# Layer 0's value products: the first 512 tokens by single blocks, norm weights spread by TensorE, one product of column group 2 moved ahead of S1

## The chip, the cores and the metric

The kernel runs on one core of one Trainium2 chip. The metric is device time in microseconds (us) of one execution. The engines are TensorE (PE), VectorE (DVE), ScalarE (ACT), GpSimd (POOL) and SyncE (SP), which issues the DMA transfers in this kernel. Each engine works through its own list of instructions in turn; semaphores tie the lists together. "SBUF" is the on-chip working memory, "PSUM" the eight banks of 128 x 512 float32 that PE writes.

## The reference

Two decoder layers on 1024 tokens of width 1024, in float32. Layer 0 mixes tokens with dilated attention in three head groups, layer 1 with gated linear attention; each is followed by a squared-ReLU MLP. What this change touches is the very beginning: the first norm and the values of layer 0.

```python
def rmsnorm(x, w):
    xf = x.astype(jnp.float32)
    y = xf * lax.rsqrt(jnp.mean(xf * xf, axis=-1, keepdims=True) + NORM_EPS)
    return (y * w.astype(jnp.float32)).astype(x.dtype)

def dilated_attention(h, w_in, w_out):
    qkv = (h @ w_in).reshape(B, S, N_GROUPS, 3, ATTN_HEADS, HEAD_DIM)
    ...
    for g, (window, dil) in enumerate(DILATED_GROUPS):
        q = apply_rope(qkv[:, :, g, 0], cos, sin) * (HEAD_DIM ** -0.5)
        k = apply_rope(qkv[:, :, g, 1], cos, sin)
        v = qkv[:, :, g, 2].astype(jnp.float32)
...
def reference(x, ...):
    for i in range(DEPTH):
        h = rmsnorm(x, norm_mix_w[i])
        ...
```

## The kernel before

**Products.** Every float32 operand is cut into a rounded part (hi, `float32r`) and a remainder (lo). A product of two operands takes three matmuls (hi by hi, hi by lo, lo by hi). Large products are split into 2 x 2 blocks and done by a scheme with seven block products instead of eight, whose operands are sums and differences of blocks. For the values (class `Values`) A is the normalized x, transposed, in four blocks: `a11` and `a12` are the first 512 tokens with the first and second half of the 1024 features, and `a21`, `a22` (tiles `a` of half 1) the tokens from 512 on. S1 = A21 + A22, S2 = S1 - A11 and so on. B is one group's 1024 x 1024 of weights; there are three groups g. `Values` counts half products n: 14 for each group, q = (n mod 14) / 2 is the block product, m the half of the contraction. Product q uses the A operand `ORDER[q]` = a12, a11, s1, s2, s4, s3, a22, so that products 0 and 1 need a12, products 2 and 3 a11, products 4 and 5 S1, and products 14 and 15 again a12, with the weights of column group 2 (g = 1). One half product is 4 token blocks x 2 x 3 = 24 matmuls of 128x128 by 512 columns; `acc` holds its four PSUM banks, pB for q = 0, 2, 4, 6 and pA for the others. `product(n, blocks)` may do it for some of the token blocks.

**Weights.** `load(n)` issues a 512 KB transfer; `rounded(n)` makes the rounded part `dh` on ACT, `remain(n)` the remainder `dl` on DVE; `total(n)` first forms a difference on DVE where the scheme needs one. `copy` moves a PSUM bank to SBUF on ACT, `add` adds another bank to it on DVE and stores the result (`vscr`). `sums(n)` calls those that stand ahead of product n.

**x.** The 8 blocks of 128 tokens come in four pairs, tiles `x0`. `Halves.norm(p)` handles a pair: ACT squares each block with a sum (`junk`, L243); `rstd_of` works out the root for both at once, with Ln and Exp on ACT (L230, L231) and five small steps on DVE; then DVE scales with the norm weights into `xn` (L252). `turn(p)` transposes the pair on PE, four 128 x 128 blocks for one PSUM bank `pT` (L334), and ACT copies each bank to the tile `a` (L336). `cut(name, c)` then makes hi on ACT (L344) and lo on DVE (L346) from `a`, 256 tokens at a time. `sum1` forms S1 (L350). The norm weights come as one transfer that repeats the row on all 128 partitions (`load_norm_w`, L208), tile `wbc`.

**Order.** In this part of the program the order is written out by hand: the sequence of calls at the end of the excerpt below is the order in which each engine gets its instructions. It goes by pairs of blocks: pair 0 is normed, transposed and cut; products 0 to 2 run on blocks 0 and 1; pairs 1 and 2 are normed; pair 1 is transposed; product 3 runs on blocks 0 and 1; then products 0 to 3 on blocks 2 and 3, S1, and the rest, one whole half product after another. Tiles come from pools of fixed size with one tag each (`h8`, `k4`, `t2`, `sm`); a buffer is used again when its readers are done.

Of the kernel before, what the change touches and what calls it, by code (L numbers as in the profile page):

```python
# [9 lines left out]
F32 = mybir.dt.float32  # L10
F32R = mybir.dt.float32r
# [3 lines left out]
OP = mybir.AluOpType  # L15
# [26 lines left out]
def hybrid_trunk(ctx, tc, x, norm_mix, norm_mlp, norm_fin, a_in, a_out, g_in, g_up, g_b, g_nw,  # L42
# [702 lines left out]
    class Values:  # L745

        STEPS = 14 * NG
        small = False
        BLOCKS = ((1, 0), (0, 0), (0, 1), (1, 1), (1, 1), None, (1, 0))

        def __init__(self):
# [78 lines left out]
                                  stop=m == 1 and k == 1 and v == 2, skip_group_check=True)  # L830

        def copy(self, name, s, t, g):
            if name == "c22":
                if t % 2 == 0:
                    self.pair = k4([P, 2, 512], F32, "c22")
# [15 lines left out]
        def sums(self, n):  # L851
# [4 lines left out]
                    self.add("c21", "B", t, g - 1)  # L856
            for t in (2 * m, 2 * m + 1):
                if q == 1:
                    self.copy("c11", "B", t, g)
# [18 lines left out]
    class Mixed(Values):  # L878

        STEPS = 28  # L880
        small = True

        def __init__(self):
            super().__init__()
# [380 lines left out]
            at(t + 10, lambda half=half: join(half), 9)  # L1265


    x0 = []
    vals = Values()
    for p in range(NB // 2):  # L1270
        t = h8([P, 2, D], F32, "x0")
        for i in range(2):
            sp.dma_start(t[:, i, :], x[0, 256 * p + 128 * i:256 * p + 128 * i + 128, :])
        x0.append(t)
        if p == 0:
            wbc = load_norm_w(norm_mix[0])
            sp.dma_start(ident, ident_d)
            for n in range(4):
                vals.load(n)
    sp.dma_start(masks, msk)  # L1280
    hs = Halves(x0, wbc, vals, None)
    hs.norm(0, (512, 768, 0, 256), 256)
# [6 lines left out]
    hs.cut("a11", 0)  # L1289
    vals.prep(2)  # L1290
    vals.prep(3)
    hs.norm(1)
    for n in range(3):
        vals.product(n, [0, 1])
    hs.norm(2)
    hs.turn(1)
    vals.product(3, [0, 1])
    hs.cut("a12", 1)
    hs.cut("a11", 1)
    vals.load(4)  # L1300
    vals.load(5)
    hs.turn(2)
    hs.sum1(0)
    vals.total(4)
    hs.rstd(3)
    hs.norm(3)
    for n in range(2):
        vals.product(n, [2, 3])
    hs.cut("s1", 0)
    vals.rounded(4)  # L1310
    hs.turn(3)
    vals.remain(4)
    vals.product(2, [2, 3])
    vals.total(5)
    vals.sums(2)
    hs.sum1(1)
    hs.cut("s1", 1)
    vals.sums(3)
    vals.rounded(5)
    vals.product(3, [2, 3])  # L1320
    vals.remain(5)
    vals.load(6)
    vals.load(7)
    for c in range(2):
# [2 lines left out]
    hs.cut("s2", 0)  # L1327
    vals.rounded(6)
    hs.cut("s2", 1)
    vals.sums(4)  # L1330
    vals.sums(5)
    vals.remain(6)
    vals.load(8)
    vals.product(4)
# [16 lines left out]
            for c in range(2):  # L1351
                hs.cut("a22", c)
    vals.load(12)
    for n in range(8, vals.STEPS):
        if n == 12:
            ctab = h8([P, 2, S], F32, "tab")
            sp.dma_start(ctab[:, 0, :], tab[:, 0, :])
# [7 lines left out]
        if n == vals.STEPS - 1:  # L1365
            heads.stage(0, 2)
            heads.stage(0, 3)
        vals.sums(n)
        vals.prep(n + 2)
        vals.load(n + 5)  # L1370
        vals.product(n)
    for t in range(4):
        vals.add("c21", "B", t, NG - 1)
# [699 lines left out]
```

## Time and profile before

| | |
|---|---|
| time, median of 3 runs | 2618.7 us (2617.86 to 2620.56) |
| the profiled execution | 2618.82 us, span 2617.0 us |
| PE busy | 2590.2 us, 99% of the span |
| DVE, ACT busy | 1859.8 us (71%), 1277.1 us (49%) |
| first product of PE starts | 12.88 us after the span's start |

The profile comes from one execution. Times on its rows count from the span's start. A row of the timeline has the start, the duration, the engine, the line, the operation and the tiles (output, then inputs), and in brackets the idle time of the engine just before, with what ended it. A row of the groups has the busy time and the mean duration in ns after the bar, then idle time. A row of the windows has, for one stretch, the busy time of PE, of PE's weight loads, DVE, ACT and POOL with the number of instructions of each, then the granted share of PE's clock, the share of the DMA engines and GB/s. A row of the waits names who waited for whom: us in total, times, longest.

### The profile page before, as it was taken

The numbers are of one execution on the slowest core, as the hardware profiler recorded it, in microseconds if no ns is written. First come the engines' busy times: TensorE is split into PE (matmuls) and PEld (weight loads), VectorE is DVE, ScalarE is ACT, GpSimd is POOL, SyncE is SP. The second block draws the span as 40 slices with busy tenths as digits, with TensorE's granted clock in tenths as the row PEclk, the third lists the DMA queues.
The fourth block names the chain that finished last, engine by engine and source line by source line (L and its number), as shares of the span: only waits on it lengthen the run. The fifth ranks groups of instructions, "written<-read, shape, count | busy, mean of one in ns | idle before, by whom it ended". The sixth has DMA issues, their size and how long they took to land.

```text
span 2617.0 us, 33041 instructions
## 1 busy us (share of the span) xinstructions
PE 2590.2 (99%) x12144; PEld 2159.1 (83%) x12144; DVE 1859.8 (71%) x2986; ACT 1277.1 (49%) x2319; POOL 1.8 (0%) x7
## 2 busy tenths in 40 slices
PE   8999999999999999999999999999999999999998
PEld 6888888888888888888888888778888888888887
DVE  7645888888888768666657587877658866666566
ACT  6333455555555436555534345654326555553343
POOL 0000000000000000000000000000000000000000
PEclk9999999999999999999999999999999999999999
DMA  5534365655656733544775452462523544396543
GB/s 189 169 129 125 101 162 133 163 151 145 160 148 172 232 121 111 179 160 146 268 263 185 139 196 96 127 205 97 176 72 127 170 147 163 127 355 202 187 147 125
DMA packets 327010, 423.12 MB, mean 162 GB/s; under 512 B 19808, under 2 KB 192224, under 8 KB 326848
## 3 DMA queue, kind: packets, MB, share of 16 engines
q1 hardware_dynamic: 326848, 421.01, 51.0%
q8 instruction: 95, 1.56, 0.2%
q14 instruction: 67, 0.55, 0.1%
HBM read 279.71 MB, written 116.06 MB: 151 GB/s over the span
## 4 chain that ended last, share of the span: by engine, by line
PE 88%; DVE 7%; ACT 3%; issue 1%; DMA 1%; SPq 0%; ACTq 0%; DVEq 0%
PE pX L598 17%; PE pB L1578 13%; PE pV L598 11%; PE pA L1578 10%; PE pY L598 6%; PE pZ L598 6%; PE pB L829 5%; PE pd L215 3%; PE pd L214 3%; PE pd L213 3%; PE pA L829 3%; PE pS L976 2%; PE pO L1017 2%; DVE dl L814 1%; PE pP L1003 1%
## 5 line engine op out<-in xcount | busy, mean ns | idle before, releaser
L1578 PE MATMUL pB<-dh 128*128 128x512 f32 x512 | 199.4, 389 | 0.0
L1578 PE MATMUL pB<-dh,dl 128*128 128x512 f32 x512 | 199.2, 389 | 0.0
L1578 PE MATMUL pB<-dl,dh 128*128 128x512 f32 x512 | 199.2, 389 | 0.0
L222 DVE TENSOR_TENSOR dl<-sin,dh 128x1024 fp32r<-128x1024 f32 x112 | 136.5, 1219 | 45.9 <-ACT dh L219 45.3
L219 ACT ACTIVATE dh<-sin 128x1024 fp32r<-128x1024 f32 x112 | 117.9, 1052 | 91.0 <-PE pB L1578 32.2
L219 ACT ACTIVATE dh<-kept 128x1024 fp32r<-128x1024 f32 x64 | 67.9, 1061 | 182.5 <-DVE kept L1543 137.8
L598 PE MATMUL pV<-s4h,wd 128*128 128x512 f32 x448 | 150.8, 398 | 0.0
L1578 PE MATMUL pA<-dh,dl 128*128 128x512 f32 x384 | 149.4, 389 | 0.0
L1578 PE MATMUL pA<-dh 128*128 128x512 f32 x384 | 149.4, 389 | 0.0
L1578 PE MATMUL pA<-dl,dh 128*128 128x512 f32 x384 | 149.4, 389 | 0.0
L992 ACT ACTIVATE pt<-pt,orow 128x128 f32<-128x128 f32 (+1 forms) x192 | 84.8, 442 | 96.7 <-DVE orow L990 96.7
L1578 PEld LDWEIGHTS pB<-dl,dh 128*128 128x128 f32 x512 | 96.1, 188 | 20.0
L1578 PEld LDWEIGHTS pB<-dh,dl 128*128 128x128 f32 x512 | 96.1, 188 | 19.9
L1578 PEld LDWEIGHTS pB<-dh 128*128 128x128 f32 x512 | 96.1, 188 | 19.8
L536 DVE TENSOR_TENSOR wal<-raw,wah 128x512 fp32r<-128x512 f32 x112 | 76.2, 687 | 42.9 <-ACT wah L535 42.9
L607 ACT ACTIVATE c<-c 128x512 f32<-128x512 f32 x64 | 40.4, 632 | 122.7 <-DVE c L635 78.9
L598 PEld LDWEIGHTS pV<-s4h,wd 128*128 128x128 f32 x448 | 84.1, 188 | 17.8 <-DVE rb L623 0.3
L536 DVE TENSOR_TENSOR wbl<-t,wbh 128x1024 fp32r<-128x1024 f32 x56 | 68.6, 1225 | 38.4 <-ACT wbh L535 38.4
L222 DVE TENSOR_TENSOR dl<-kept,dh 128x1024 fp32r<-128x1024 f32 x64 | 78.3, 1224 | 24.5 <-ACT dh L219 18.6
L990 DVE CUSTOM_DVE_ANT_0 pt<-pS,masks 128x128 f32<-128x128 f32 (+1 forms) x192 | 58.2, 347 | 50.5 <-PE pS L976 50.5
L598 PE MATMUL pY<-a12h,wah 128*128 128x512 f32 x224 | 89.5, 400 | 0.0
L598 PE MATMUL pZ<-a22h,wgh 128*128 128x512 f32 x224 | 89.3, 399 | 0.0
(336 smaller groups left out, 7370.5 us busy)
## 6 DMA issues: line engine op xcount, KB each, us to landing
sin<-acts SPq DMA_DIRECT2D x112, 512.0 KB, 3.9
raw<-in_mlp_w_up_dram SPq DMA_DIRECT2D x64, 512.0 KB, 5.8
acts<-s SPq DMA_DIRECT2D x64, 512.0 KB, 3.4
raw<-in_mlp_w_down_dram SPq DMA_DIRECT2D x64, 512.0 KB, 4.7
raw<-in_attn_w_in_dram SPq DMA_DIRECT2D x96, 256.0 KB, 4.5
cw<-c SPq DMA_DIRECT2D x192, 128.0 KB, 2.3
acts<-c SPq DMA_DIRECT2D x64, 256.0 KB, 2.1
kept<-in_mlp_w_down_dram SPq DMA_DIRECT2D x32, 512.0 KB, 5.7
```

What stands on the lines that cost most here:

```text
L213: pe.matmul(ps, sh, mh, start=start, stop=False)
L214: pe.matmul(ps, sh, ml, start=False, stop=False)
L215: pe.matmul(ps, sl, mh, start=False, stop=stop)
L219: act.activation(hi, src, AF.Copy)
L222: dve.tensor_tensor(lo, src, hi.bitcast(F32), op=OP.subtract)
L536: self.remain(lambda: dve.tensor_tensor(lo, src, hi.bitcast(F32), op=OP.subtract))
L598: pe.matmul(st[b], u[:, k, :], v, start=first and k + n == 0, stop=k == 3 and n == 2, skip_group_check=True)
L829: pe.matmul(self.acc[s][t], a[:, c], b[:, k, :], start=fresh and m + k + v == 0, stop=m == 1 and k == 1 and v == 2, skip_group_check=True)
L976: pe.matmul(ps[:, i, :128 * n], self.qT[:, 128 * b:128 * b + 128], self.kT[:, k0:k0 + 128 * n], start=True, stop=True)
L990: dve.tensor_tensor_reduce(pt[:, i, :128 * n], ps[:, i, :128 * n], masks[:, m0:m0 + 128 * n], -scale, 1e38, op0=OP.add, op1=OP.min, accum_ ...
L992: act.activation(pt[:, i, :128 * n], pt[:, i, :128 * n], AF.Exp, scale=-1.0, bias=m, accum_out=self.row[:, r, HD:HD + 1])
L1578: pe.matmul(self.acc[s][t], a[:, k, c], b[:, k, :], start=fresh and m + k + v == 0, stop=m == 7 and k == 1 and v == 2, skip_group_check=True)
```

## The change

**Blocks.** The first 512 tokens are handled one block of 128 at a time. `root(b)` forms the reciprocal root of one block with two steps less on DVE; `normed(b, half)` scales one half of its features; `facing(b, half)` transposes this half, four 128 x 128 blocks into one bank, and ACT rounds hi straight from that bank. Its `rest()` makes lo on DVE from the bank as well, and then ACT copies the bank to `a`. Products 0 to 3 run block by block (`both`), and each block's c11 is copied and added at once.

**Norm weights.** The row of norm weights is loaded once, to one partition (`wrow`, 4 KB). PE spreads it over the partitions, two matmuls with a row of ones; DVE copies the two banks to `wbc`.

**Column group 2.** Products 14 and 15 (a12 by the weights of g = 1) run block by block after products 0 to 3, ahead of S1. Their results, c11 of g = 1, are copied at once to two pair tiles and kept until product 18. The list of the later steps (`plan`) leaves 14 and 15 out. Blocks 4 to 7 are transposed by `turn` as before, but their roots and scalings stand among these steps.

**Transfers.** Order before: blocks 0 and 1, the spread norm weights, ident, weights 0 to 3, the other blocks, masks. Now: block 0, the row of norm weights, ident, weights 0 to 2, block 1, weights 3, blocks 2 to 5, weights 14 and 15, blocks 6 and 7, masks. Weights 4 and 5 follow the stores of c11.

```diff
         def copy(self, name, s, t, g):
-            if name == "c22":
+            if name == "c22" or (name == "c11" and g == self.ahead):
...
+    def root(b):
+        r = root0[b] = sm([P, 5], "root")
+        ss, nv, t, y, z = (r[:, i:i + 1] for i in range(5))
+        junk = t2([P, D], BF16, "junk")
+        act.activation(junk, rows0(b), AF.Square, accum_out=ss)
+        dve.tensor_scalar(nv, ss, -0.5 / D, -0.5 * EPS, op0=OP.mult, op1=OP.add)
+        act.activation(t, ss, AF.Ln, scale=1.0 / D, bias=eps)
+        act.activation(y, t, AF.Exp, scale=-0.5)
+        dve.scalar_tensor_tensor(z, y, nv, y, op0=OP.mult, op1=OP.mult)
+        dve.scalar_tensor_tensor(z, z, 1.5, y, op0=OP.add, op1=OP.mult)
...
+    def facing(b, half):
+        ps = bank("pT").rearrange("p (k t) -> p k t", k=4)
+        for k in range(4):
+            c = 512 * half + 128 * k
+            pe.transpose(ps[:, k, :], xn0[b][:, c:c + 128], ident)
+        s, sl = vals.h[("a11", "a12")[half]], slice(128 * b, 128 * b + 128)
+        hi, lo = s.hi[0][:, :, sl], s.lo[0][:, :, sl]
+        act.activation(hi, ps, AF.Copy)
+
+        def rest():
+            dve.tensor_tensor(lo, ps, hi.bitcast(F32), op=OP.subtract)
+            act.activation(hs.a[0, half][0][:, :, sl], ps, AF.Copy)
+        return rest
...
+    for c in (512, 0):
+        ps = bank("pw")
+        pe.matmul(ps, ones[0:1, 0:P], wrow[0:1, c:c + 512], start=True, stop=True)
+        dve.tensor_copy(wbc[:, c:c + 512], ps)
+    root(0)
+    normed(0, 1)
     vals.rounded(0)
-    hs.turn(0, (2, 3))
+    rest = facing(0, 1)
     vals.remain(0)
-    hs.cut("a12", 0)
-    hs.turn(0, (0, 1))
-    vals.prep(1)
...
+    for b in range(1, 4):
+        rest = facing(b, 0)
+        both(0, b)
+        rest()
+        vals.add("c11", "A", b - 1, 0)
+        root(b + 1)
+        if b < 3:
+            normed(b + 1, 1)
+            rest = facing(b + 1, 1)
+            vals.copy("c11", "B", b, 0)
+            both(2, b)
+            rest()
+            normed(b + 1, 0)
+        else:
+            vals.rounded(14)
+            root(5)
+            normed(4, 1, 0)
+            vals.remain(14)
+            normed(5, 1, 0)
+            vals.copy("c11", "B", b, 0)
+            both(2, b)
+    hs.xn[2] = [xn0.pop(4), xn0.pop(5)]
+    hs.turn(2)
+    vals.prep(15)
+    root(6)
+    both(14, 0)
+    vals.add("c11", "A", 3, 0)
+    root(7)
+    normed(6, 1, 0)
+    hs.sum1(0)
+    normed(7, 1, 0)
+    hs.cut("s1", 0)
+    vals.copy("c11", "B", 0, 1)
+    both(14, 1)
...
-    for n in range(8, vals.STEPS):
+    plan = [*range(8, 14), *range(16, vals.STEPS), *range(vals.STEPS, vals.STEPS + 5)]
+    for i, n in enumerate(plan[:-5]):
```

The order of instructions at two places. On ACT, from the squares of one group of blocks to the copies after the next transposes, before (pT is a bank of transposes, junk the squares, t and y the root, a the transposed x; a bracket names the engines or transfers whose semaphores the row waits for):

```order
L243 ACTIVATE junk_258,ss_257<-x0_110 128x1024 [waits DMAHW2_49]
L243 ACTIVATE junk_260,ss_257<-x0_110 128x1024 [waits DMAHW3_49]
L230 ACTIVATE t_264<-v_262 128x2 [waits DVE_49]
L231 ACTIVATE y_263<-t_264 128x2 [waits Activation_49]
L336 ACTIVATE a_144<-pT_278 128x2x256 [waits PE_49]
L336 ACTIVATE a_145<-pT_284 128x2x256 [waits PE_49]
L336 ACTIVATE a_144<-pT_290 128x2x256 [waits PE_49]
L336 ACTIVATE a_145<-pT_296 128x2x256 [waits PE_49]
L344 ACTIVATE a12h_160<-a_145 128x4x256 [waits Activation_49]
L344 ACTIVATE a11h_180<-a_144 128x4x256
```

and now, one turn of the loop over blocks (b = 1):

```order
L1331 ACTIVATE a11h_128<-pT_234 128x4x128 [waits PE_49]
L1335 ACTIVATE a_130<-pT_234 128x4x128 [waits DVE_49]
L1310 ACTIVATE junk_257,root_256<-x0_94 128x1024 [waits DMAHW0_49]
L1312 ACTIVATE root_256<-root_256,eps_100 128x1 [waits Activation_49]
L1313 ACTIVATE root_256<-root_256 128x1 [waits Activation_49]
L1331 ACTIVATE a12h_126<-pT_266 128x4x128 [waits PE_49]
L840 ACTIVATE c11_272<-pB_164 128x512
L1335 ACTIVATE a_131<-pT_266 128x4x128 [waits DVE_49]
L1331 ACTIVATE a11h_128<-pT_289 128x4x128 [waits PE_49]
```

Before, the squares of pair 2 stand ahead of pair 1's transposes, and every copy of a bank waits for PE alone. Now the squares of block 2 stand behind the copy of block 1's bank, and that copy waits for DVE, whose remainder reads the same bank.

On DVE, the steps from the roots to the scaling of tokens from 512 on (v, t, y or root the reciprocal root, xn the scaled block, x0_110 and x0_95 the pair with blocks 4 and 5), before:

```order
L229 TENSOR_SCALAR v_262<-ss_257 128x2
L232 TENSOR_TENSOR t_264<-y_263 128x2
L233 TENSOR_TENSOR t_264<-t_264,v_262 128x2
L234 TENSOR_SCALAR t_264<-t_264 128x2
L235 TENSOR_TENSOR y_263<-y_263,t_264 128x2
L252 SCALAR_TENSOR_TENSOR xn_272<-x0_110,y_263,wbc_96 128x512
L252 SCALAR_TENSOR_TENSOR xn_273<-x0_110,y_263,wbc_96 128x512
L252 SCALAR_TENSOR_TENSOR xn_272<-x0_110,y_263,wbc_96 128x512
L252 SCALAR_TENSOR_TENSOR xn_273<-x0_110,y_263,wbc_96 128x512
L346 TENSOR_TENSOR a12l_161<-a_145,a12h_160 128x4x256
```

and now:

```order
L845 TENSOR_TENSOR c11_327<-pA_207,c11_327 128x512
L1311 TENSOR_SCALAR root_366<-root_366 128x1
L1314 SCALAR_TENSOR_TENSOR root_366<-root_366 128x1
L1315 SCALAR_TENSOR_TENSOR root_366<-root_366 128x1
L1311 TENSOR_SCALAR root_376<-root_376 128x1
L1314 SCALAR_TENSOR_TENSOR root_376<-root_376 128x1
L1315 SCALAR_TENSOR_TENSOR root_376<-root_376 128x1
L1322 SCALAR_TENSOR_TENSOR xn_384<-x0_95,root_366,wbc_98 128x512
L1322 SCALAR_TENSOR_TENSOR xn_384<-x0_95,root_366,wbc_98 128x512
L815 TENSOR_TENSOR dl_387<-raw_119,dh_374 128x1024
L1322 SCALAR_TENSOR_TENSOR xn_389<-x0_95,root_376,wbc_98 128x512
L1322 SCALAR_TENSOR_TENSOR xn_389<-x0_95,root_376,wbc_98 128x512
```

Before, the scaling of blocks 4 and 5 alternates between the two and stands ahead of the remainders of blocks 2 and 3. Now both roots stand ahead of block 4's scaling, behind the sum of c11 for block 2, and the remainder of weights 14 stands between the two blocks.

More of the change, by code (lines that the diff above doesn't have):

```diff
@@ L1292, in hybrid_trunk @@
[L1292 to L1299, printed above, removed]
+    rest()
+    normed(0, 0)
+    vals.rounded(1)
+    vals.product(0, [0])
+    rest = facing(0, 0)
+    vals.remain(1)
+    vals.product(1, [0])
+    vals.rounded(2)
+    rest()
+    vals.remain(2)
+    root(1)
+    normed(1, 1)
+    vals.rounded(3)
+    vals.product(2, [0])
+    rest = facing(1, 1)
+    vals.remain(3)
@@ L1307, in hybrid_trunk @@
[L1307 to L1315 removed]
+    vals.rounded(4)
     hs.sum1(1)
     hs.cut("s1", 1)
[L1318 removed]
+    vals.remain(4)
+    vals.copy("c11", "B", 2, 1)
+    vals.total(5)
     vals.rounded(5)
[L1320 removed]
+    both(14, 3)
     vals.remain(5)
+    vals.copy("c11", "B", 3, 1)
     vals.load(6)
```

81 lines of the change are left out of this document (56 added, 25 removed).

## The prediction

> **What bounds the kernel now.** The page says at once who sets the time: TensorE is busy for nearly all of the span.
>
> ```profile
> span 2617.0 us, 33041 instructions
> PE 2590.2 (99%) x12144; PEld 2159.1 (83%) x12144; DVE 1859.8 (71%) x2986; ACT 1277.1 (49%) x2319; POOL 1.8 (0%) x7
> ```
>
> So a change can only act where TensorE (PE) does not run at its pace. The windows by stage show where that is.
>
> ```profile
> 0.00:13.00 13.00, 3.98 (x17) 3.28 (x17) 5.36 (x15) 7.46 (x12) 0.20 (x4) 1.00 0.88 305
> 13.00:30.00 17.00, 16.30 (x82) 12.88 (x83) 14.74 (x25) 14.89 (x27) 0.00 (x0) 1.00 0.84 307
> 30.00:50.00 20.00, 19.04 (x89) 14.92 (x88) 17.87 (x29) 13.72 (x25) 0.00 (x0) 1.00 0.00 1
> 50.00:80.00 30.00, 29.47 (x130) 23.94 (x129) 26.18 (x33) 16.28 (x22) 0.00 (x0) 1.00 0.39 123
> 80.00:120.00 40.00, 40.00 (x178) 33.11 (x177) 21.77 (x26) 12.17 (x16) 0.00 (x0) 1.00 0.63 211
> ```
>
> From 80 us on PE is never idle, and a pipelined product of 512 columns takes 40.00/178 = 0.225 us. In the first 50 us VectorE (DVE) is busy for up to nine tenths (17.87 of 20.00), and ScalarE (ACT) for up to 14.89 of 17.00. The waits of PE name what it lacks, and the timeline gives the two ends of the stage: its first product, and the starts of product 4 and product 6 (the half products are counted from 0).
>
> ```profile
> PE pT L334 <- DVE xn L252: 10.3, 7, 8.9
> 12.88 0.80 PE L829 MATMUL pB<-dh,a12h 128*128 128x512 f32 x1
> 27.98 1.91 PE L334 MATMUL pT<-ident,xn 128*128 128x128 f32 x16
> 44.52 0.39 PE L829 MATMUL pB<-dh,s1h 128*128 128x512 f32 x1
> 55.40 0.39 PE L829 MATMUL pA<-dh,s2h 128*128 128x512 f32 x1
> 66.10 1.15 DVE dl L814
> 67.29 10.95 PE pB L829 x47
> ```
>
> Products 4 and 5 have 48 matmuls between 44.52 and 55.40: 0.2267 us each. The transposes cost 1.91/16, less the 0.27 tail of the last, 0.11 each. By 44.52 PE has done the 96 matmuls of products 0 to 3 and 64 transposes, 21.8 + 7.0 = 28.8 us of work. It has lost 44.5 - 28.8 = 15.7 us, most of it before 12.88. The chain shows one more loss, where PE waits for dl until 67.29: 0.8. **PE loses 16.5 us in this stage; the change does the same products and transposes, so it is worth 16.5 minus what PE loses afterwards.**
>
> **The change part by part.** Prices of single steps, by group over the first 70 us:
>
> ```profile
> L334 PE MATMUL pT<-ident,xn 128*128 128x128 f32 x64 | 11.0, 316 | 10.6 <-DVE xn L252 10.3 <-ACT a L336 0.3
> L336 ACT ACTIVATE a<-pT 128x512 f32<-128x512 f32 x16 | 8.7, 597 | 2.3 <-PE pT L334 2.3
> L243 ACT ACTIVATE junk<-x 128x1024 bf16<-128x1024 f32 x8 | 8.4, 1057 | 2.6 <-DMA x<-in_x_dram 2.5
> L243 ACT ACTIVATION_READ_ACCUMULATOR junk<-x 128x1 f32 x8 | 1.6, 198 | 0.0
> L230 ACT ACTIVATE t<-v 128x2 f32<-128x2 f32 x4 | 0.8, 203 | 2.3 <-DVE v L229 2.3
> L234 DVE TENSOR_SCALAR t<-t 128x2 f32<-128x2 f32 x4 | 0.7, 170 | 0.1
> L252 DVE SCALAR_TENSOR_TENSOR xn<-x,y,wbc 128x512 f32<-128x512 f32 x12 | 8.2, 746 | 0.1
> L346 DVE TENSOR_TENSOR s1l<-s,s1h 128x512 fp32r<-128x512 f32 x4 | 2.6, 685 | 0.1
> L808 ACT ACTIVATE dh<-raw 128x1024 fp32r<-128x1024 f32 x4 | 4.2, 1060 | 1.7 <-DMA raw<-in_attn_w_in_dram 1.7
> L814 DVE TENSOR_TENSOR dl<-raw,dh 128x1024 fp32r<-128x1024 f32 x4 | 4.9, 1220 | 0.7 <-ACT dh L808 0.7
> ```
>
> In round figures: a copy or rounding of 512 columns on ACT 0.60, a block's squares with their sum 1.2, Ln and Exp 0.4 together, the two DVE steps of the root with their hops 0.4, half a block scaled on DVE 0.75, a remainder of 512 columns 0.68, dh 1.06 and dl 1.22 (each about 0.1 less where the next instruction overlaps it).
>
> *Start to the first product.* The first block of x is first in the queue in both kernels. The rows below give its landing, the first transposes, and the first weights' landing (the release of dh).
>
> ```profile
> 4.54 1.06 ACT L243 ACTIVATE junk<-x 128x1024 bf16<-128x1024 f32 x1 [2.53 <-DMA x<-in_x_dram]
> 8.95 3.86 PE L334 MATMUL pT<-ident,xn 128*128 128x128 f32 x16 [8.95 <-DVE xn L252]
> 9.24 1.06 ACT L808 ACTIVATE dh<-raw 128x1024 fp32r<-128x1024 f32 x1 [1.66 <-DMA raw<-in_attn_w_in_dram]
> L976 PE MATMUL pS<-kT,qT 128*128 128x256 f32 x176 | 45.9, 379 | 0.0
> L976 PE MATMUL pS<-kT,qT 128*128 128x128 f32 x208 | 32.3, 273 | 0.0
> ```
>
> The weights lose the 512 KB of spread norm weights and the second block of x ahead of them, and land well before they are needed. The spreading is new: two float32 matmuls of 512 columns. None is in the trace. In the nearest rows 128 further columns cost (379 - 273) = 106 ns, and 384 records for 192 score matmuls mean two passes each, so 2 x 4 x 0.106 = 0.85 at full clock; the first transposes go at 3.86/16 = 0.24, half the later pace, so 1.7 each as the other end. I take 1.7, since they run at the very start, from 4.5 when the row of weights lands with the first block. DVE copies each half out (0.69), and both copies stand ahead of the first block's root on DVE: 4.5 + 1.7 + 1.7 + 0.7 = 8.6, the root's last steps to 8.8, half a block scaled 9.6, four slow transposes 10.8, rounded 11.4. So the first product starts 1.5 us earlier than at 12.88, not much more.
>
> *The rest of block 0.* What follows that product is a single file of small steps: remainder 0.7, copy 0.6, dh 1.0, dl 1.2 (14.9); a11's rounding after its transposes, remainder, copy (17.1); squares 1.2, Ln and Exp 0.4, root 0.4, half scaled 0.75 (19.9); transposes 0.7, rounding 0.6, remainder 0.7, half scaled 0.7, transposes 0.5: 23.1. By then PE has done 24 matmuls and 16 transposes, 7.2 us: **15.9 lost**.
>
> *The loop over blocks 1 to 3.* After the transposes of a first half PE has one pair of half products, 12 x 0.227 = 2.7 us. The next transposes need rounding 0.6, remainder 0.7, copy 0.6, squares 1.2, Ln and Exp 0.4, root 0.4, half scaled 0.75 after those transposes: 4.7 and some hops, 4.9. PE stands 2.15 us, twice: **4.3 lost**. The copy into `a` waits for the remainder, as the order shows with its wait on DVE; no row of before has two engines reading one bank, so its price is bounded by nothing and by the remainder's 0.68 per round; I take 0.68, because the wait is in the program.
>
> [...]
>
> *Block 4 to 7.* On DVE the roots of blocks 4 and 5 now stand ahead of the scaling of block 4, and dl of product 14 ahead of that of block 5. From block 3's transposes on: 0.6 + 0.7 + 0.6 + 1.2 + 0.4, dh 1.0, squares 1.2, Ln and Exp 0.4, root 0.4, two halves 1.4 make 7.9, against 5.4 of products: 2.4 lost. Then dl 1.1 and two halves 1.4 before the second operand of the same transposes: 2.35 lost. Product 15 is cut only after the four copies of these transposes, 4 x 0.5, then dh 1.06 and dl 1.22, against 1.6 of transposes and 1.4 of matmuls: 1.7 lost. Block 7's scaling follows the two sums of S1 (1.3): 1.9 lost. Later 0.3. **Together 8.65.**
>
> The loads of weights 4 and 5 now follow the four stores of c11 on SP; block 3's sum frees them near 57, a load takes about 4, and the product needs them near 67: nothing. The pair tile that now holds c11 of group 1 and the later steps shifted by two products cost nothing, since PE is never idle after 80 us.
>
> Sum: 15.9 + 4.3 + 8.65 = 28.85 lost, against 16.5: **12.3 us slower**.
>
> *The clock.* This stretch of before is the nearest to those stalls:
>
> ```profile
> 862.00:864.00 2.00, 0.77 (x6) 0.39 (x5) 2.00 (x9) 1.06 (x5) 0.00 (x0) 1.00 0.16 36
> 864.00:866.00 2.00, 2.00 (x9) 1.83 (x10) 1.97 (x6) 1.55 (x6) 0.00 (x0) 0.61 0.77 167
> 866.00:868.00 2.00, 2.00 (x6) 1.53 (x6) 1.97 (x4) 0.60 (x1) 0.00 (x0) 0.54 0.51 127
> ```
>
> After 2 us with PE 0.77 busy the granted clock fell to 0.61 and 0.54 of two windows: (0.39 + 0.46) x 2 = 1.7 us of PE lost. The double stall before block 4 leaves PE nearly idle for 4.8 us, so I count one such fall there, at half its 1.7 because ACT's copies set the pace then: 0.9. [...]
>
> The profiled execution took 2618.82 (span 2617.0 and 1.8 around it), beside a median of 2618.7. 2618.8 + 12.3 + 0.9 = 2632.0.
>
> **The rivals.** *Everything hides (faster).* The place is ACT between a block's transposes and the next ones. If that chain fitted into the 2.7 us of the block's products there, PE would wait for nothing after its first product; with the spreading at full clock that starts at 9.7, and PE would lose 9.3 in all, 7.2 less than before: 2611.6. It decides at 2.7 us against the 4.9 of the rows; for it speaks that ACT has idle time in the 70 us, against it that the order puts the squares behind the copy. 0.04. *The roots hide, the rest does not.* If ACT and DVE take the squares and roots earlier than I read from the order, the loop's two stalls and the double one before block 4 go with the clock's fall: 4.3 + 4.75 + 0.9 less, 2622.0, which is within what a measurement can tell. Against it: each engine works its list in turn. 0.08. *The clock falls at every stall.* Each 2.15 us stall leaves a window as empty as the quoted one; two more falls at 1.7: 2635.4. For it speaks the quoted fall, against it that a stall of 2.15 us may straddle two windows. 0.25, a part of slower. *The start is not earlier*, because the row of weights lands late: another 1 to 2 us. 0.1, also slower.
>
> **How the numbers follow.** The forecast has 0.53; it, the clock and the late start make slower 0.88. From 2632.0 the low end takes the fast spreading (1.7 less), no clock fall (0.9) and the wait on the remainder gone with smaller hops (2.4): 2627.0. The high end takes two more falls and a late start: 2637.0. About 0.2 per cent, 5.2 us, is what a measurement of this kernel tells from no change.
>
> **What would show it.** The first L830 product near 11.4; PE waits on xn of about 2.1 us twice, near 28 and 36, with the copy into `a` and the squares ahead of them on ACT; a pair of waits near 48 and 50; PE without idle time from 72 on, some 13 us behind. I am wrong if PE's waits for xn total less than 8 us, or if PE falls behind after 80 us.

## The result, and the profile after

The changed kernel takes **2636.35 us** (median of 5 runs, 2635.63 to 2637.27) beside 2618.7 for the kernel before (5 runs, 2617.86 to 2620.56): 17.65 us more, a ratio of **1.0068, 95% interval 1.0058 to 1.0079**. The forecast was 2632.0 in a range of 2627.0 to 2637.0: slower, as it turned out, with the size inside the range and 4.35 us short. The profiled execution took 2636.35.

The head of the page after, whose PE row has the four passes of the spreading more (12148 against 12144):

```profile
span 2634.5 us, 33069 instructions
PE 2598.3 (99%) x12148; PEld 2162.5 (82%) x12148; DVE 1862.1 (71%) x2993; ACT 1280.2 (49%) x2331; POOL 2.0 (0%) x8
```

The windows by stage (length, then busy time with instructions of PE, PEld, DVE, ACT and POOL, then the granted clock, the DMA share and GB/s), to be held against those of before:

```profile
0.00:13.00 13.00, 6.05 (x11) 2.83 (x12) 4.98 (x10) 5.07 (x8) 0.40 (x5) 1.00 0.86 307
13.00:30.00 17.00, 13.02 (x53) 9.03 (x52) 9.62 (x17) 10.40 (x20) 0.00 (x0) 0.95 0.59 228
30.00:50.00 20.00, 17.47 (x71) 13.73 (x70) 7.24 (x16) 10.68 (x22) 0.00 (x0) 0.87 0.07 27
50.00:80.00 30.00, 23.15 (x105) 18.87 (x106) 21.98 (x36) 16.73 (x32) 0.00 (x0) 0.89 0.29 97
80.00:120.00 40.00, 40.00 (x177) 32.89 (x176) 33.80 (x41) 21.81 (x29) 0.00 (x0) 1.00 0.38 111
```

From 80 to 120 us PE has no idle time, and its idle time after that is the same as before's (given further below), so the loss is made ahead of 80 us. Between 13 and 80 us PE issues 229 instructions where before it issued 301, and two numbers say why: PE is busy less, and the granted clock, 1.00 in every one of before's windows, is 0.95, 0.87 and 0.89. (The record of the clock begins with its first rise, here at 14.71; ahead of that a row shows 1.00 although the matmuls stand 0.43 us apart, from 12.40 to 12.83, and 0.23 later.) DVE, the engine that was busy for nine tenths in before's third window, is busy for 7.24 of 20.00: nothing is full, each engine waits for the others. The waits of PE name whom it waits for (us in total, times, the longest):

```profile
PE pT L1328 <- DVE xn L1322: 7.2, 5, 2.2
PE pT L334 <- DVE xn L1322: 6.6, 3, 2.5
```

That is 13.8 us of waiting for scaled blocks, against 10.3 in before, of which 8.9 was the start. One turn of the loop on ACT and DVE, from the timeline (start, duration, engine, line, operation, and in brackets the idle time before it with its releaser):

```profile
24.95 0.60 ACT L1335 ACTIVATE a<-pT 128x512 f32<-128x512 f32 x1 [0.76 <-DVE a11l L1334]
25.44 1.05 ACT L1310 ACTIVATE junk<-x 128x1024 bf16<-128x1024 f32 x1
26.61 0.29 ACT L1312 ACTIVATE root<-root,eps 128x1 f32<-128x1 f32 x1
27.43 0.16 DVE L1315 SCALAR_TENSOR_TENSOR root<-root 128x1 f32<-128x1 f32 x1
27.62 0.75 DVE L1322 SCALAR_TENSOR_TENSOR xn<-x,root,wbc 128x512 f32<-128x512 f32 x1
28.43 1.11 PE L1328 MATMUL pT<-ident,xn 128*128 128x128 f32 x4 [2.13 <-DVE xn L1322]
```

The copy waits for DVE's remainder, the squares for the copy, the root for the squares, the scaling for the root and PE's transposes for the scaling, one after the other; PE stands 2.13 us. The next rows are windows of 3.41 us, the length of the shortest stretch at half clock, cut so that the clock's changes fall on their ends:

```profile
24.95:28.36 3.41, 1.35 (x6) 0.77 (x5) 1.83 (x5) 2.13 (x5) 0.00 (x0) 1.00 0.20 77
28.36:31.77 3.41, 3.34 (x10) 2.86 (x11) 1.36 (x3) 1.68 (x3) 0.00 (x0) 0.50 0.00 0
35.19:38.60 3.41, 1.41 (x7) 0.82 (x5) 1.83 (x6) 2.13 (x5) 0.00 (x0) 1.00 0.21 77
38.60:42.01 3.41, 3.30 (x10) 2.82 (x11) 1.41 (x3) 1.68 (x3) 0.00 (x0) 0.50 0.00 0
48.84:52.25 3.41, 0.93 (x5) 0.42 (x3) 2.10 (x6) 1.82 (x5) 0.00 (x0) 1.00 0.01 5
52.25:55.67 3.42, 1.30 (x7) 1.15 (x7) 2.22 (x3) 0.21 (x1) 0.00 (x0) 0.50 0.00 0
55.67:59.08 3.41, 3.41 (x15) 3.12 (x14) 0.00 (x0) 2.64 (x5) 0.00 (x0) 0.50 0.00 0
```

Each of the three stalls is followed by a stretch at half clock: 13.65 us in all, in which PE is busy for 3.34 + 3.30 + 1.30 + 3.41 = 11.35 us. Half of that is 5.7 us; the forecast had 0.9 for it.

### The profile page after: what moved, and what is told of

Its sections match the earlier page's. It is cut to its first block, busy times and chain, and to the rows that moved or that the text cites. A ratio compares the mean times of both kernels' runs of the same rounds, so it can differ in the third digit from the quotient of the medians.

```text
span 2634.5 us, 33069 instructions
## 1 busy us (share of the span) xinstructions
PE 2598.3 (99%) x12148; PEld 2162.5 (82%) x12148; DVE 1862.1 (71%) x2993; ACT 1280.2 (49%) x2331; POOL 2.0 (0%) x8
## 4 chain that ended last, share of the span: by engine, by line
PE 81%; DVE 12%; ACT 4%; issue 2%; DMA 1%; SPq 0%; ACTq 0%; DVEq 0%
PE pX L598 14%; PE pB L1680 13%; PE pA L1680 10%; PE pV L598 9%; PE pB L830 5%; PE pY L598 5%; PE pZ L598 4%; PE pA L830 4%; PE pd L215 3%; PE pd L214 3%; PE pd L213 3%; PE pS L979 2%; PE pO L1020 2%; PE pP L1006 1%; DVE dl L815 1%
```

## The experiments

Two things were to be told apart: whether the stalls come from the order of ACT's and DVE's steps or from what the new steps cost, and how much of the loss is the stalls themselves and how much the clock. All medians, each with the kernel before on the same chip:

| run | median, us | before beside it | ratio (95%) | above before |
|---|---|---|---|---|
| changed kernel | 2636.35 | 2618.7 | 1.0068 (1.0058 to 1.0079) | 17.65 |
| roots early | 2625.18 | 2617.86 | 1.0030 (1.0019 to 1.0041) | 7.3 |
| PE kept busy | 2632.46 | 2617.86 | 1.0054 (1.0041 to 1.0068) | 14.6 |
| weights by DMA | 2633.51 | 2617.86 | 1.0061 (1.0048 to 1.0073) | 15.65 |
| bank read once | 2633.32 | 2617.86 | 1.0058 (1.0046 to 1.0071) | 15.5 |
| root before spreading | 2633.30 | 2617.62 | 1.0057 (1.0045 to 1.0070) | 15.7 |
| no product ahead | 2645.63 | 2617.62 | 1.0105 (1.0091 to 1.0119) | 28.0 |
| three together | 2622.41 | 2617.62 | 1.0017 (1.0008 to 1.0026) | 4.8 |
| pairs, product ahead | 2614.83 | 2618.15 | 0.9987 (0.9978 to 0.9997) | -3.3 |
| changed kernel again | 2635.45 | 2618.25 | 1.0064 (1.0052 to 1.0077) | 17.2 |
| no fall at all | 2631.89 | 2618.25 | 1.0050 (1.0037 to 1.0064) | 13.6 |

An interval is some 2.7 us to either side, so the four runs at 14.6 to 15.7 are not parted from the changed kernel by their times alone; what follows from them rests on their traces.

**The roots at the start of a loop turn.**

```diff
     for b in range(1, 4):
+        root(b + 1)
+        if b == 3:
+            root(5)
         rest = facing(b, 0)
         both(0, b)
         rest()
         vals.add("c11", "A", b - 1, 0)
-        root(b + 1)
...
-            root(5)
```

> The squares and root of the next block are issued at the start of each loop turn, ahead of the first half's transposes and their copies; nothing is left out. Theory (the single file of ACT and DVE steps makes PE stand, and each stall makes the clock fall): squares 1.2, Ln and Exp 0.4 and root 0.4 leave the chain of 4.9 us between two sets of transposes, so 2.9 stands against 2.7 of products: the two loop stalls go from 2.3 to under 0.8 us each, the pair before block 4 from 5.0 to under 3.5 together, and the three stretches at half clock between 28 and 59 us go or shrink to one. Time 2624 to 2629. Rival (the loss is in the start and the single file of block 0): the stalls from 28 us on shrink but the time stays above 2633, since PE is then late elsewhere. Rival (the squares were not what held the transposes, the remainder and the copy were): stalls stay above 1.6 us each, time 2633 to 2636.

Measured 2625.18, 7.3 above before where the changed kernel was 17.65: more than half of the loss is where the three ACT steps of a root stand in its row. The same chain in this run's timeline:

```profile
23.50 1.06 ACT L1310 ACTIVATE junk<-x 128x1024 bf16<-128x1024 f32 x1
25.12 0.58 ACT L1331 ACTIVATE a11h<-pT 128x512 fp32r<-128x512 f32 x1
26.94 0.74 DVE L1322 SCALAR_TENSOR_TENSOR xn<-x,root,wbc 128x512 f32<-128x512 f32 x1
27.73 0.66 PE L1328 MATMUL pT<-ident,xn 128*128 128x128 f32 x4 [1.12 <-DVE xn L1322]
34.50 0.66 PE L1328 MATMUL pT<-ident,xn 128*128 128x128 f32 x4 [0.18 <-DVE xn L1322]
```

The squares now run at 23.50, ahead of the rounding; the scaling at 26.94 no longer waits for a root, and PE waits 1.12 and 0.18 in place of 2.13 and 2.12. The first of the two is more than the 0.8 that the theory allowed: block 1's rounding, at 25.12, now stands behind block 2's squares. The pair of waits before block 4 shrinks to one of 1.88 us between matmul starts; that before block 7, 2.16, stays. The profiled execution, 2627.25, is the slowest of this kernel's seven: it has one stretch at half clock, from 57.14 to 60.55. Both rivals fall.

**PE kept busy in the stalls.** What is added computes nothing that is used:

```diff
     def facing(b, half, idle=0):
         ps = bank("pT").rearrange("p (k t) -> p k t", k=4)
+        if idle:
+            dh = vals.cut[0][0]
+            for _ in range(idle):
+                pe.matmul(ps..., dh[:, 0, 0:P], dh[:, 1, :], start=True, stop=True, ...)
...
-            rest = facing(b + 1, 1)
+            rest = facing(b + 1, 1, 9)
...
-    hs.turn(2)
+    hs.turn(2, idle=21)
```

> Matmuls that compute nothing needed are put into the stalls (9 before the transposes of a second half in the loop, 21 before block 4's first transposes), with the stalls themselves left as they are; the output is the same. Theory: the transposes still start when xn arrives, as late as before, but PE's clock stays at full speed through 60 us, where after had 13.7 us at half clock. The time falls by what the clock cost, 3 to 5.5 us: 2631 to 2633.5, and what remains against before, about 12 to 14 us, is the stalls alone. Rival (as in the forecast: ACT's copies set the pace there, so half a clock costs nearly nothing): the clock is full and the time stays 2635 to 2636.5. Rival (the clock does not follow how busy PE is): the half clock stays where it was, and the time with it or later.

Measured 2632.46. The transposes after the first stall start at 28.71 (28.43 in the changed kernel), so the stall is there as before, and the three stretches at half clock are gone. But the wait before blocks 6 and 7, which was not filled, now has one (63.98 to 67.39), which the changed kernel did not. So this run gives only a lower bound, and on another chip than the changed kernel. The two runs that close this section take up both.

**The weights of the norm by DMA.**

```diff
-    sp.dma_start(wrow[0:1, :], bass.AP(..., ap=[[D, 1], [1, D]]))
+    sp.dma_start(wbc, bass.AP(..., ap=[[0, P], [1, D]]))
...
-    for c in (512, 0):
-        ps = bank("pw")
-        pe.matmul(ps, ones[0:1, 0:P], wrow[0:1, c:c + 512], start=True, stop=True)
-        dve.tensor_copy(wbc[:, c:c + 512], ps)
```

> The norm weights come as the 512 KB load that repeats the row for every partition, as in before, in place of the row and the two float32 matmuls with their copies; all else as after. Theory: the start hardly changes the whole, since the first block's root is nearly done when the weights land: the first product moves by under 1 us either way, the later loads shift by about 1.3 us, and the stalls from 28 us on stay: 2634 to 2637. Rival (the spreading at the slow clock of the first microseconds, and the row that lands after the first block of x, cost several us): 2629 to 2632. Rival (the spreading is worth the 1.5 us by which the forecast had the first product earlier): 2637 to 2639.

Measured 2633.51, in the range of neither the theory (from 2634) nor the rival (up to 2632), and the theory was wrong on the start: it has the first product move by under 1 us. Five rows of the changed kernel (the sum of the first block's squares, the second copy of spread weights, the root's first step on DVE, the first transposes and the first product), and the last three of these in this run:

```profile
5.29 0.18 ACT L1310 ACTIVATION_READ_ACCUMULATOR junk<-x 128x1 f32 x1
7.88 0.69 DVE L1345 COPY wbc<-pw 128x512 f32<-128x512 f32 x1 [1.02 <-PE pw L1344]
8.49 0.14 DVE L1311 TENSOR_SCALAR root<-root 128x1 f32<-128x1 f32 x1
10.01 1.12 PE L1328 MATMUL pT<-ident,xn 128*128 128x128 f32 x4 [2.16 <-DVE xn L1322]
11.81 0.79 PE L830 MATMUL pB<-dh,a12h 128*128 128x512 f32 x1 [0.69 <-ACT a12h L1331]
```

```profile
5.32 0.15 DVE L1310 TENSOR_SCALAR root<-root 128x1 f32<-128x1 f32 x1 [4.46 <-ACT junk L1309]
7.27 1.12 PE L1327 MATMUL pT<-ident,xn 128*128 128x128 f32 x4 [7.27 <-DVE xn L1321]
9.59 0.80 PE L830 MATMUL pB<-dh,a12h 128*128 128x512 f32 x1 [1.20 <-ACT a12h L1330]
```

The first product comes 2.2 us earlier without the spreading. In the changed kernel the root's sum is ready at 5.5, but its first step on DVE runs at 8.49, behind the second copy of the spread weights. Whether PE's four passes or the place of the copies costs this is what the next run but one asks.

**The bank read once.**

```diff
-        act.activation(hi, ps, AF.Copy)
+        a = hs.a[0, half][0][:, :, sl]
+        act.activation(a, ps, AF.Copy)
+        act.activation(hi, a, AF.Copy)
 
         def rest():
-            dve.tensor_tensor(lo, ps, hi.bitcast(F32), op=OP.subtract)
-            act.activation(hs.a[0, half][0][:, :, sl], ps, AF.Copy)
+            dve.tensor_tensor(lo, a, hi.bitcast(F32), op=OP.subtract)
```

> The transposes are copied from their bank into a first, and the rounded and the remaining part are then made from a; so the bank has one reader, and no engine waits for the other's read of it. All else as after. Theory: only the remainder's 0.7 us leaves the chain between two sets of transposes (rounding and copy stay on ACT): the loop stalls go from 2.3 to about 1.6 us, the time by 1.5 to 3.5 us, the more if one of the clock's falls goes with them: 2632.5 to 2635. Rival (the wait of one engine for the other's read of the bank is the main cost): stalls under 0.8 us, 2624 to 2629. Rival (the longer way to the rounded part costs the products as much as the wait): 2635.5 to 2638.

Measured 2633.32. The copies into a among the groups of the first 80 us, in the changed kernel:

```profile
L1335 ACT ACTIVATE a<-pT 128x512 f32<-128x512 f32 x8 | 4.8, 596 | 4.3 <-DVE a11l L1334 2.3 <-DVE a12l L1334 2.0
```

and in this run, with the two stalls of the loop from its timeline:

```profile
L1332 ACT ACTIVATE a<-pT 128x512 f32<-128x512 f32 x8 | 4.8, 597 | 15.6 <-PE pT L1328 15.6
29.59 0.66 PE L1328 MATMUL pT<-ident,xn 128*128 128x128 f32 x4 [1.44 <-DVE xn L1322]
37.89 0.66 PE L1328 MATMUL pT<-ident,xn 128*128 128x128 f32 x4 [1.45 <-DVE xn L1322]
```

The copies no longer wait for DVE, and the loop's waits go from 2.13 to 1.45. So the second reader of a bank costs 0.68 a round, as the forecast took it, and with waits of 1.44 and 1.45 the granted clock stays at 1.00 in the loop, from 25.17 to 42.24 us. The gain stays small, since the first product now waits for copy and rounding (12.43 against 11.81), and a stretch at half clock is left in the opening (52.48 to 55.90).

**The first block's root before the copies.**

```diff
+    spread = []
     for c in (512, 0):
         ps = bank("pw")
         pe.matmul(ps, ones[0:1, 0:P], wrow[0:1, c:c + 512], start=True, stop=True)
-        dve.tensor_copy(wbc[:, c:c + 512], ps)
+        spread.append(ps)
     root(0)
+    dve.tensor_copy(wbc[:, 512:D], spread[0])
     normed(0, 1)
+    dve.tensor_copy(wbc[:, 0:512], spread[1])
```

> The spreading of the norm weights by TensorE stays, but on DVE the first block's root now stands ahead of the two copies that take the spread weights from their banks, and the second copy stands behind the first half's scaling; all else as after. Theory (the start is late because those copies, at 6.2 and 7.9 us in after, stand ahead of a root whose sum was ready at 5.5): the first transposes go from 10.0 to 7.6 to 8.2 us, the first product from 11.8 to about 9.3 to 9.8, and of these 2 us the whole keeps what the load of the weights by DMA kept: 2633 to 2635. Rival (the matmuls of the spreading at the slow clock, four passes of 0.85 us, hold the start by themselves): the first transposes stay above 9.3 us, the time above 2635.5. Rival (the start does not matter since the stalls from 28 us on swallow what it gains): first product near 9.5, time 2635.5 to 2637.

```profile
5.27 0.15 DVE L1311 TENSOR_SCALAR root<-root 128x1 f32<-128x1 f32 x1 [4.41 <-ACT junk L1310]
7.69 1.12 PE L1328 MATMUL pT<-ident,xn 128*128 128x128 f32 x4
9.50 0.79 PE L830 MATMUL pB<-dh,a12h 128*128 128x512 f32 x1 [0.69 <-ACT a12h L1331]
```

Measured 2633.30, and the first product at 9.50, as early as with the load by DMA (9.59). Against that load the spreading costs the start nothing; two copies that stood in DVE's row ahead of a root which was ready cost 2.3 us there. The profile of this run has one more stretch at half clock than the changed kernel's: its granted clock from 50 to 80 us is 0.83, beside 0.89.

**No product ahead.** Products 14 and 15 go back behind group 1:

```diff
-        ahead = 1
+        ahead = None
...
-    both(14, 0)
...
-    both(14, 3)
...
-    plan = [*range(8, 14), *range(16, vals.STEPS), ...]
+    plan = [*range(8, vals.STEPS + 5)]
```

> The product of column group 2 (14 and 15) goes back to its place after group 1, as in before, with its loads and copies; the single blocks, the rounding from the banks and the spreading stay as in after. Theory (its 48 matmuls, 10.9 us, are the only work PE has while ACT and DVE make blocks 5 to 7 and S1, so this part of the change pays): PE stands for 8 to 12 us more between 50 and 75 us, and the time rises to 2642 to 2648. Rival (as the forecast priced it: the rounding and remainders of 14 and 15 are what delays blocks 4 to 7, 2.35 and 1.7 us of its sum): without it the time falls to 2632 to 2635. Rival (neither, the two cancel): 2635 to 2638.

Measured 2645.63, 28.0 above before: this part of the change is worth 10 us to the changed kernel. The window of 50 to 80 us, and the transposes of blocks 6 and 7, which now find PE with nothing to do:

```profile
50.00:80.00 30.00, 16.05 (x58) 12.75 (x59) 20.98 (x35) 14.11 (x26) 0.00 (x0) 0.66 0.33 114
61.79 0.45 PE L334 MATMUL pT<-ident,xn 128*128 128x128 f32 x1 [5.75 <-DVE xn L1319]
```

PE is busy for 16.05 of 30.00 us, at a clock of 0.66. The forecast booked what 14 and 15 take from ACT and DVE and used their matmuls as cover for that; it did not price that without them PE would have had next to no work there.

**Three orders together.** The two edits of order above, and in blocks 4 to 7:

```diff
             vals.rounded(14)
-            root(5)
-            normed(4, 1, 0)
+            normed(4, 1)
+            normed(5, 1)
+            normed(4, 0)
+            normed(5, 0)
             vals.remain(14)
-            normed(5, 1, 0)
...
+    vals.rounded(15)
+    root(6)
     hs.xn[2] = [xn0.pop(4), xn0.pop(5)]
-    hs.turn(2)
-    vals.prep(15)
-    root(6)
+    hs.turn(2, (2, 3, 0, 1))
+    vals.remain(15)
```

The run also puts the sum of c11 for block 2 behind the remainder of 14, and the root and scaling of block 7 ahead of the sums of c11 for block 3 and of S1.

> After with three orders changed and the same instructions: the root of the next block at the start of each loop turn, the first block's root ahead of the copies of the spread weights, and for blocks 4 to 7 the four scalings ahead of the remainders of 14 and 15, with 15 rounded before the transposes of blocks 4 and 5. Theory (what the change loses is the order of ACT's and DVE's steps, not the steps): the gains of the single edits add up, 11.2 for the roots, about 2.5 for the start and 1 to 2 for blocks 4 to 7: 2620 to 2623, with no stretch at half clock or one. It stays above before's 2618, since single blocks still make PE wait 0.3 to 1.0 us at eight places before 25 us. Rival (the gains share one cause and don't add): 2624 to 2626. Rival (with the order mended the change pays, as its product ahead gives PE work where before had 3 us of waits): below 2617.

Measured 2622.41: 12.9 of the 17.65 us come back with no instruction fewer, and the clock is at 1.00 through the whole opening. PE's waits for xn are 2.8 us in place of 13.8:

```profile
PE pT L1328 <- DVE xn L1322: 1.9, 3, 1.1
PE pT L334 <- DVE xn L1322: 0.9, 1, 0.9
```

The gains nearly add: 10.3 and 2.0 from the single edits, 1 to 2 expected for blocks 4 to 7. What stays is the single file of block 0 and, halfway through the transposes of blocks 6 and 7, a wait of 1.4 us that ends with ACT's copy of c11.

**Before's pairs with the product ahead.** The last two runs say which part of the change costs and which pays; so the part that pays was put into the kernel before:

```diff
-        def turn(self, p, pairs=(0, 2, 1, 3)):
+        def turn(self, p, pairs=(0, 1, 2, 3)):
...
-    hs.turn(1)
-    vals.product(3, [0, 1])
+    vals.product(3, [0])
+    hs.turn(1)
+    vals.product(3, [1])
...
-    hs.turn(3)
...
     vals.product(2, [2, 3])
+    vals.prep(14)
     vals.sums(2)
+    vals.sums(3)
+    hs.turn(3)
     hs.sum1(1)
     hs.cut("s1", 1)
+    vals.prep(15)
...
+    vals.product(14)
+    vals.product(15)
```

> Before's pairs of blocks, with its loads of the norm weights and its rounding from a, and of the change only the product of column group 2 ahead of S1; with that work at hand for PE, the transposes of blocks 6 and 7 move behind product 2, those of blocks 2 and 3 behind half of product 3, and a pair's transposes go in the order in which DVE makes their columns. Theory (the product ahead is the part of the change that pays, the single blocks are the part that costs): PE's waits of before at 22 to 24, 35 to 38 and 67 us go but for some 0.4 us, 3 to 3.7 us in all: 2613.5 to 2615.5, faster than before. Rival (the four copies of c11 of group 1, the later sums or the loads of 14 and 15 among the first blocks of x take it back): 2616.5 to 2619. Rival (the product ahead pays only beside single blocks): above 2619.

Measured 2614.83 beside 2618.15: a ratio of 0.9987 (0.9978 to 0.9997), faster than both kernels, by little but with the interval below one. The windows of its opening:

```profile
13.00:30.00 17.00, 16.44 (x77) 13.28 (x77) 13.64 (x25) 14.10 (x25) 0.00 (x0) 1.00 0.83 317
30.00:50.00 20.00, 19.76 (x99) 16.45 (x98) 17.65 (x26) 14.84 (x27) 0.00 (x0) 1.00 0.16 53
50.00:80.00 30.00, 30.00 (x134) 24.85 (x133) 26.87 (x35) 18.44 (x26) 0.00 (x0) 1.00 0.38 123
```

PE is busy 19.76 of 20.00 and 30.00 of 30.00, where before had 19.04 and 29.47; its only wait of the opening for xn is that of the start (9.3 us). How much of the 3.3 us comes from the product ahead and how much from the moved transposes is not shown: those of blocks 2 and 3, 16 in 2.95 us in before (22.17 to 25.12) where 16 without waits take about 1.8, were freed of their waits by half of product 3, and before with the moves alone was not tried.

**The clock's price, on one chip.** The changed kernel again, and beside it the run with PE kept busy with 9 more idle matmuls before blocks 6 and 7:

```diff
     hs.xn[3] = [xn0.pop(6), xn0.pop(7)]
-    hs.turn(3)
+    hs.turn(3, idle=9)
```

> The changed kernel itself, on the chip of the run beside it, so that the two are compared without a chip between them. Every theory expects 2635.5 to 2637.5, with the three stretches at half clock after the stalls near 28, 38 and 52 us (3.4, 3.4 and 6.8 us long).

> As the run with PE kept busy, with 9 more matmuls that compute nothing needed before the transposes of blocks 6 and 7, where that run still had one stretch at half clock; the stalls stay. Theory (the clock's falls are what the forecast had too small): no half clock from 17 to 100 us, and against the changed kernel beside it 4 to 6 us less, that is the 5.7 us which half a clock took from 11.35 us of busy PE, less what a faster PE then waits for the remainder of product 15 (up to 0.8 more than the 0.9 there): 2630.5 to 2632.5, and what stays against before, 12.5 to 14.5 us, is the stalls. Rival (the forecast's 0.9 was right and some other cost hides behind it): 2634.5 to 2636.

The changed kernel gave 2635.45, just under its range, and this one 2631.89, 13.6 above before. The clock is full in all of the opening:

```profile
30.00:50.00 20.00, 19.93 (x94) 16.21 (x93) 9.70 (x21) 11.26 (x24) 0.00 (x0) 1.00 0.08 28
50.00:80.00 30.00, 28.78 (x140) 23.00 (x139) 23.29 (x37) 17.80 (x32) 0.00 (x0) 1.00 0.33 114
```

The difference, 3.6 us, is a little under the 4 to 6 that were expected, while the time is in the range given for it. Four times the forecast's 0.9, it is less than the 5.7 counted from the windows, for two reasons. Part of the half clock lay on time that PE would have waited anyway: with the clock full, product 15 waits 1.6 us for its rounding and remainder, where it waited 0.9 while the transposes ran slowly. And some of the gain is given back later. The start of product 6 in the changed kernel beside it, and in this run:

```profile
85.88 0.39 PE L830 MATMUL pA<-dh,s2h 128*128 128x512 f32 x1
```

```profile
81.25 0.39 PE L834 MATMUL pA<-dh,s2h 128*128 128x512 f32 x1
```

That is 4.6 us for the clock in the opening, of which 3.9 is left at the end of the two spans (2634.2 and 2630.3).

## Why the forecast was right, and which term was too small

*Start to the first product*: forecast 11.4, measured 11.81, from the same steps (the row of weights landed at 4.1, the passes took 0.85 each). What the step did not see is that the two copies ahead of the root cost 2.3 us which the new order gave away: an earlier start was there to be had.

*The rest of block 0*: the transposes that end it start at 22.90 and end at 23.3, forecast 23.1. With 7.2 us of work done by then, 16.1 are lost, forecast 15.9.

*The loop over blocks 1 to 3*: 2.29 and 2.28 lost between matmul starts, forecast 2.15 twice. The chain was right step by step, down to the copy that waits for the remainder. Without the remainder's wait (0.68) both stalls shortened by that; without the squares and root (2.0) the second wait shortened by 1.9 and the first by 1.0, as another rounding then stood behind the squares.

*Block 4 to 7*: stalls of 2.64 before the first transpose of block 4 and 2.35 before that of block 5, 0.88 at product 15 and 2.12 before block 7's first transpose, 8.0 in all, forecast 8.65.

```profile
52.07 0.34 PE L334 MATMUL pT<-ident,xn 128*128 128x128 f32 x1 [2.48 <-DVE xn L1322]
54.52 3.46 PE L334 MATMUL pT<-ident,xn 128*128 128x128 f32 x15 [2.12 <-DVE xn L1322]
67.12 1.86 PE L334 MATMUL pT<-ident,xn 128*128 128x128 f32 x15 [1.96 <-DVE xn L1322]
```

The 1.7 for product 15 was too much here, since the slow transposes covered half of it; at full clock it is 1.6.

So the stalls add to 16.1 + 4.57 + 8.0 = 28.7 where the forecast had 28.85, and 28.7 - 16.5 = 12.2 us is what it had as 12.3. The run without a fall of the clock, 13.6 above before (9.7 to 16.8 by its interval), agrees.

*The clock* is the term that was mis-sized: one fall at 0.9 us, where three stalls were followed by a fall, of 3.41, 3.41 and 6.83 us, at a price of 3.6 us against the kernel beside it. That is 2.7 of the 4.35 us which part 2636.35 from the forecast; the rest is less than the interval of either comparison. The case was in the prediction, as the rival in which the clock falls at every stall, with 0.25 and 2635.4; that is nearer to the measured time than the forecast, which lies inside its range only because the high end took in two more falls and a late start that did not come. The step that failed is the weighing of the rival's evidence: the one row of before with a fall had PE busy for 0.77 of 2.00 us, and in the windows of 3.41 that hold the loop's stalls PE was busy for 1.35 and 1.41: shares of 0.40 and 0.41 beside that row's 0.39. It was held that a stall may straddle two windows; in the changed kernel's profile all but 0.1 us of either loop stall (26.30 to 28.43, 36.59 to 38.71) lay in one, and as a turn of the loop takes 10.28 us (28.43 to 38.71), three windows, the second lies in its window where the first did. That a stall can straddle, the same profile shows later: the waits of 1.07 and 0.16 us at 863.5 and 864.0 after which before fell to half clock stand at 882.3 and 882.8 there, the first across the end of a window at 881.69: PE is busy for 2.55 and 2.69 us in the two windows, where the one of before from 861.02 to 864.43 had 2.02 of 3.41, and no fall follows.

*What was said to hide* did. The prediction's "never idle after 80 us" holds as far as its row goes, to 120 us; later PE does wait in both kernels, and as much: to the end of the span it is idle for 15.9 of 2554.5 us, and in before for 15.6 of 2537.0. The loads of weights 4 and 5 behind the stores delayed no product.

The timeline gives the sum once more. Product 6 starts here:

```profile
85.42 0.39 PE L830 MATMUL pA<-dh,s2h 128*128 128x512 f32 x1
```

Before, it started at 55.40. The 48 matmuls of products 14 and 15 that now stand ahead of it are 10.9 us; 85.42 - 55.40 - 10.9 = 19.1, less what before still loses at 67.29 (0.7 between matmul starts, 66.37 and 67.29, where the prediction had 0.8): 18.4. At the end 17.5 of it is left (spans of 2634.5 and 2617.0); part of the difference is before's stretch at half clock from 864 us, which the profile after does not have.

What stays open: the times alone do not part the runs on the weights, the bank and the first root from the changed kernel, so their prices (about 2 us each) are read from traces and single comparisons; the two readers of one bank were not tried without the wait; and the moved transposes were not tried without the product ahead.

## What to carry to other kernels

When one engine is busy for 99 per cent, a change of order elsewhere is worth what it does to that engine's few waits, so write the chain of the other engines from one wait to the next, with each instruction's place in its row, and compare it with the work at hand. Smaller blocks start sooner but leave less work to cover a chain that does not shrink with them (2.7 us of products against 4.9); giving the waiting engine other ready work (the product ahead, 10 us) or issuing the long step earlier in the turn (the roots, 10 us) was worth far more than any single instruction. And price a stall twice: once for its length, and once for the clock after it (here 3.6 us in all for the half clock in the opening).

## What the runs showed of the hardware

In the profiles of the two kernels the record of the granted clock changes only at whole multiples of 3.413 us from its first rise (14.51 us in before, 14.71 in the changed kernel): it falls at 864.43 and rises at 867.84 in the one, falls at 28.36, 38.60 and 52.25 and rises at 31.77, 42.01 and 59.08 in the other, and both fall once more 5 us ahead of the span's end. Cut into windows of that length up to 2600 us (ahead of the first rise counted back from it and taken as half clock, as the matmuls' spacing says there), each window's work was counted from the matmul records at their spacing when they follow one another without a wait (0.227 us for a product matmul of 512 columns; 0.11 for 128 columns in float32, which a transpose is, and 0.22 for 256), twice that at half clock. The four windows at full clock that were followed by half clock had shares of 0.35, 0.37 and 0.21 (the changed kernel, from 24.95, 35.19 and 48.84) and 0.36 (before, from 861.02). The 1505 that were followed by full clock had 0.48 or more. The six windows at half clock that were followed by full clock had 0.83 or more. Windows with 0.34 (the changed kernel, from 52.25) and 0.58 (before, from 7.68) were followed by half clock again, and so was one of the changed kernel, from 4.47 to 7.88, in which PE was busy for 3.38 of 3.41 us with the passes of the spreading; why it was is not shown. So the loop's waits of 2.13 and 2.12 us, each but for 0.1 us within one window, were both followed by a fall; in the run that reads the bank once the second wait, 1.45 within the window from 35.41 to 38.82, left PE busy for 1.96 of 3.41 us, and no fall followed. The busy time of the profile, which holds the tails of the matmuls (0.39 us where the next one starts after 0.227), shows this less sharply than the count: a window of before with 2.02 of 3.41 us (from 861.02) was followed by a fall, one of the run with the roots early with 1.71 of 3.42 (from 43.48) was not.

The spreading's float32 matmuls with 512 columns show four passes in the trace, two for each half of the weights; they start at 4.10, 5.08, 5.94 and 6.79 us, 0.85 apart but for the first two (0.98), the upper of the forecast's two ends (1.7 for two).
